# Attention scores of two heads together, with the low key part on 64 rows of the array per head

## The chip, the cores and the metric

The program runs on one core of one Trainium2 chip. The metric is the device time of one execution in microseconds (us), as the median of several runs. TensorE (PE) multiplies; it loads weights in instructions of its own (PEld in the profile). VectorE (DVE), ScalarE (ACT) and GpSimd (POOL) work beside it, and SyncE (SP) issues most of the DMAs.

## What is computed

A network of two transformer blocks and a third mixer, on 1024 tokens of width 1024. The first block has a windowed attention (layer A below: 16 query heads on 4 key heads, a band of 128 keys to each side, and a sink), the second a dilated attention (layer B: three groups of 8 query heads on 2 key heads, dilations 1, 4 and 16). Each is followed by a gated feed-forward net, and then comes a mixer of a state-space model and a short convolution. What matters here is the scores in the attentions, cut from the reference:

```python
def banded_attention(q, k, v, half_window, slopes, dist_scale, sink=None):
    ...
    s = jnp.einsum('nbqhgd,nbkhd->nbhgqk', qb, kw,
                   preferred_element_type=jnp.float32) * (dh ** -0.5) + bias
    s = jnp.where(mask[None, :, None, None], s, NEG)
    m = s.max(axis=-1)
    ...
    p = jnp.exp(s - m[..., None])
    l = p.sum(axis=-1)
    ...
    o = jnp.einsum('nbhgqk,nbkhd->nbqhgd', p, vw.astype(jnp.float32))
```

A head has 64 channels (`dh`), so a score is a sum over 64 products.

## The kernel before

**Two parts for each number.** All large products are made in fp32r, with each operand cut into a high part and the rest, the low part. Projections take three products (`mm3`, L571 to L578: high by high, high by low, low by high).

**Scores.** As a head has 64 channels and the array 128 rows, both parts of a query stand in one tile: `Q[i]` has the high part on rows 0 to 63 and the low part on rows 64 to 127 (written in `q_proj`, L682 and L686). `K1` has the high part of the keys on both halves of the rows, `K2` the low part on both. So two matmuls into one PSUM bank make a head's scores (`Block.score`, L113 and L114): `Q` by `K1` gives high by high plus low by high, and `Q` by `K2` gives high by low plus low by low. The query tile of 128 by 128 is the weight; 192, 256 or 384 columns of keys stream past it. All 128 rows are used in both matmuls.

**Blocks.** A `Block` is 128 queries of four heads that share their keys. Layer A has 32 blocks (4 key heads by 8), with 384 keys, and 256 in the first and last block of a key head. Layer B has 48 (6 units by 8), with 256 keys, and 192 in the first and last block of a unit of dilation 1. So there are 80 blocks, 320 heads, and 640 score matmuls. After its scores, a head goes through DVE (L117: PSUM plus bias into SBUF, with the maximum), ACT (L126: exponential, with the sum), in layer A POOL (L136: division by the sum), PE again (L756: transposes into PSUM), ACT and DVE (L759, L760: the two parts of the weights `pt`) and PE (L770: product with the values `V`). The scores' PSUM banks have the tag `sc`, of which there are two.

**Order.** `attend` (L709) issues the scores of heads 0 and 1, then some matmuls of a projection that has nothing to do with the block (`fill`; lines L590 to L592 and, in the end of layer A, L821 to L823), the scores of heads 2 and 3, the transposes of the block before, and so on. A scheduler then sets the final order of each engine's instructions from priorities and its own estimates, and can put a matmul of another chain between two score matmuls. In the last blocks of layer B there is hardly anything to fill with.

**Matmuls on 64 rows** are already there in small number. The transposes of the values (L658) read rows 64 to 127, and in the first and last block of a unit of dilation 1 the product with the 64 outer values (`vx`, in L770) uses rows 0 to 63. In the order of the kernel before there are 20 stretches of matmuls on fewer than 128 rows.

Of the kernel before, what the change touches and what calls it, by code (L numbers as in the profile page):

```python
# [28 lines left out]
def fl(t):  # L29
    return t.bitcast(F32)  # L30
# [65 lines left out]
class Block:  # L96
# [10 lines left out]

    def score(self, i):

        nc, w, s = self.net.nc, self.w, self.ss[i]  # L110
        ps = self.net.bank("sc")
        keys = slice(self.k0, self.k0 + self.n)
        nc.tensor.matmul(ps[:, 0:self.n], self.Q[i], self.K1[:, keys], start=True, stop=False)  # L113
        nc.tensor.matmul(ps[:, 0:self.n], self.Q[i], self.K2[:, keys], start=False, stop=True)  # L114
        if self.e:
            nc.gpsimd.tensor_copy(s[:, w:w + 1], self.sink[:, i:i + 1])
        nc.vector.tensor_tensor_reduce(s[:, 0:w], ps[:, self.m0:self.m0 + w], self.bias[i], 1.0,  # L117
                                       self.sink[:, i:i + 1] if self.e else -3.0e38, op0=ALU.add, op1=ALU.max,
                                       accum_out=self.mx[:, i:i + 1])
        if i == 3:  # L120
            self.nm = self.net.small([P, 4], "nm", 3)
            nc.vector.tensor_scalar_mul(self.nm, self.mx, -0.125)  # L122
# [26 lines left out]
class Net:  # L149
# [520 lines left out]
    def q_proj(self, Ws, h, perm, Q, halves_first=False, soon=None):  # L670

        nc = self.nc
        for t, hf in [(t, hf) for hf in range(2) for t in range(2)] if halves_first else [(0, 0), (0, 1), (1, 0), (1, 1)]:
            ps = self.bank("g")
            for _ in self.col_gemm_steps(ps, Ws[t](), h, hf):
                yield
                if soon:
                    soon()
                    soon = None
            src = [perm(ps[64 * i:64 * i + 64], None) for i in range(2)]  # L680
            for i in range(2):
                nc.scalar.copy(perm(Q[2 * t + i][0:64], hf), src[i])  # L682
            yield
            for i in range(2):
                q = Q[2 * t + i]
                nc.vector.tensor_sub(perm(q[64:128], hf), src[i], perm(fl(q[0:64]), hf))  # L686

    def project(self, W, h, perm, res, wide, v_tiles, halves_first=False):

# [19 lines left out]
    def attend(self, blocks, fill):  # L709


        last = None
        for n, block in enumerate(blocks + [None]):
            b = block and block()
            if b:
                b.score(0)
                b.score(1)
            fill(n, 0)
            if b:
                b.score(2)  # L720
                b.score(3)
            if last:
                last.turn()
                last.turn()
            if b:
                b.soft(0)
                b.soft(1)
            fill(n, 1)
            if last:
                last.turn()  # L730
            if b:
                b.soft(2)
                b.soft(3)
            fill(n, 2)
            if b and b.e:
                b.weigh()
            if last:
                last.apply()
            last = b
# [1334 lines left out]
```

## Time and profile before

| | |
|---|---|
| Median of 3 runs | 2753.62 us (2752.54 to 2756.7) |
| The profiled execution | 2757.76 us, with a span of 2756.0 us |
| PE busy over the span | 2593.1 us (94%) |
| Granted TensorE clock, mean | 0.980 |
| Layer A attention, 85 to 390 us | 305 us, PE busy in 290.77 |
| Layer B attention, 1185 to 1535 us | 350 us, PE busy in 316.41 |

The other stages (feed-forward nets, the third mixer) run no score matmul. Matmuls are pipelined: a matmul's time in the profile reaches to the end of its last result, while the next has long begun. What a matmul costs in a full stream is the time from its start to the start of the next one, which is why the rows below are read by their starts.

### The profile page before, as it was taken

The numbers are of one execution on the slowest core, as the hardware profiler recorded it, in microseconds if no ns is written. First come the engines' busy times: TensorE is split into PE (matmuls) and PEld (weight loads), VectorE is DVE, ScalarE is ACT, GpSimd is POOL, SyncE is SP. The second block draws the span as 40 slices with busy tenths as digits, with TensorE's granted clock in tenths as the row PEclk, the third lists the DMA queues.
The fourth block names the chain that finished last, engine by engine and source line by source line (L and its number), as shares of the span: only waits on it lengthen the run. The fifth ranks groups of instructions, "written<-read, shape, count | busy, mean of one in ns | idle before, by whom it ended". The sixth has DMA issues, their size and how long they took to land. (4 is left out here: it accounts for less than half of the span.)

```text
span 2756.0 us, 33954 instructions
## 1 busy us (share of the span) xinstructions
PE 2593.1 (94%) x11966; PEld 2115.1 (77%) x11966; DVE 1899.1 (69%) x3559; ACT 1286.1 (47%) x2416; POOL 376.4 (14%) x506
## 2 busy tenths in 40 slices
PE   4999998999999999988899889999999899999998
PEld 4777676888888788776787668888887777988877
DVE  7788777977775976755667798666656978165355
ACT  4577743433333345568888443333333445123131
POOL 2255521000000000023343200000000102020000
PEclk8999999999999999999999999999999999999999
DMA  7333341544444666311122414222274565161141
GB/s 276 99 93 96 119 123 69 156 142 146 138 138 139 232 200 194 107 39 40 39 55 78 145 59 146 82 86 83 85 244 150 176 199 175 54 180 52 46 144 63
DMA packets 283403, 336.74 MB, mean 122 GB/s; under 512 B 59384, under 2 KB 212704, under 8 KB 282592
## 3 DMA queue, kind: packets, MB, share of 16 engines
q1 hardware_dynamic: 277520, 315.59, 36.4%
q0 software_dynamic: 5312, 18.88, 2.1%
q8 instruction: 94, 1.54, 0.2%
q14 instruction: 77, 0.63, 0.1%
q10 hardware_dynamic: 400, 0.09, 0.0%
HBM read 265.14 MB, written 67.27 MB: 121 GB/s over the span
## 5 line engine op out<-in xcount | busy, mean ns | idle before, releaser
L1188 PE MATMUL psg<-H,wpart 128*128 128x512 f32 x2112 | 504.6, 393 | 14.3 <-ACT H L432 10.0
L1188 PEld LDWEIGHTS psg<-H,wpart 128*128 128x128 f32 x2112 | 397.8, 189 | 103.6 <-ACT H L432 12.8
L1175 ACT CAST wpart<-wraw 128x512 fp32r<-128x512 f32 x264 | 163.3, 622 | 248.3 <-PE pstp L1188 76.4
L1188 PE MATMUL pssc<-H,wpart 128*128 128x512 f32 x1056 | 255.0, 390 | 0.5 <-DVE ev L1208 0.5
L1188 PEld LDWEIGHTS pssc<-H,wpart 128*128 128x128 f32 x1056 | 198.1, 188 | 42.1 <-DVE ev L1208 0.9
L1176 DVE TENSOR_TENSOR wpart<-wraw,wpart 128x512 fp32r<-128x512 f32 x264 | 180.9, 686 | 68.5 <-ACT wpart L1175 66.7
L1325 PE MATMUL psg<-part,wpart 128*128 128x512 f32 x792 | 206.8, 394 | 8.0 <-DVE wpart L1291 3.1
L1325 PE MATMUL pssc<-part,wpart 128*128 128x512 f32 x792 | 207.4, 394 | 5.2 <-DVE ev L1212 3.6
L590 PE MATMUL psg<-hh,wh 128*128 128x512 f32 x480 | 198.5, 414 | 2.2 <-ACT hh L527 1.7
L1290 ACT CAST wpart<-wraw 128x640 fp32r<-128x640 f32 (+1 forms) x132 | 101.0, 765 | 210.7 <-PE psg L1325 101.8
L591 PE MATMUL psg<-hl,wh 128*128 128x512 f32 x480 | 192.6, 401 | 2.0 <-DVE hl L530 1.9
L592 PE MATMUL psg<-hh,wl 128*128 128x512 f32 x480 | 191.8, 400 | 0.0
L1325 PEld LDWEIGHTS psg<-part,wpart 128*128 128x128 f32 x792 | 148.4, 189 | 42.7 <-DVE part L1297 5.5
L126 ACT ACTIVATE s<-s,nm 128x256 f32<-128x256 f32 (+4 forms) x320 | 162.4, 511 | 39.6 <-DVE nm L122 33.1
L1325 PEld LDWEIGHTS pssc<-part,wpart 128*128 128x128 f32 x792 | 148.3, 189 | 39.4 <-DVE ev L1212 4.3
L1291 DVE TENSOR_TENSOR wpart<-wraw,wpart 128x640 fp32r<-128x640 f32 (+1 forms) x132 | 117.7, 892 | 83.4 <-ACT wpart L1290 75.8
L1203 ACT COPY ev<-psg 128x512 f32<-128x512 f32 x132 | 77.4, 588 | 205.1 <-PE psg L1188 141.0
L780 POOL TENSOR_TENSOR o<-o,ob 64x512 f32<-64x512 f32 x80 | 117.3, 1467 | 231.8 <-ACT o L779 221.6
L403 POOL TENSOR_TENSOR nacc<-nacc,nsq 128x512 f32<-128x512 f32 x30 | 40.5, 1350 | 761.8 <-ACT nsq L401 761.5
L1325 PE MATMUL pstp<-part,wpart 128*128 128x512 f32 x528 | 137.9, 393 | 0.0
L1296 ACT CAST part<-a 128x512 fp32r<-128x512 f32 x176 | 108.5, 618 | 58.0 <-PE pssc L1325 17.7
L1297 DVE TENSOR_TENSOR part<-a,part 128x512 fp32r<-128x512 f32 x176 | 119.6, 691 | 19.0 <-ACT part L1296 17.8
(454 smaller groups left out, 5488.8 us busy)
## 6 DMA issues: line engine op xcount, KB each, us to landing
adaw<-in_ada_w_dram SPq DMA_DIRECT2D x96, 512.0 KB, 4.2
wraw<-in_ffn_w_in_dram SPq DMA_DIRECT2D x88, 512.0 KB, 3.9
a<-acts SPq DMA_DIRECT2D x132, 256.0 KB, 4.0
acts<-ev SPq DMA_DIRECT2D x44, 512.0 KB, 2.7
wraw<-in_ffn_w_out_dram SPq DMA_DIRECT2D x44, 384.0 KB, 3.5
xs<-x SPq DMA_DIRECT2D x32, 512.0 KB, 3.5
x<-xs SPq DMA_DIRECT2D x32, 512.0 KB, 5.1
wraw<-in_ffn_w_out_dram SPq DMA_DIRECT2D x44, 320.0 KB, 3.3
```

Source lines behind the costliest of these rows:

```text
L126: self.net.nc.scalar.activation(s[:, 0:w], s[:, 0:w], AF.Exp, bias=self.nm[:, i:i + 1], scale=0.125, accum_out=self.l[:, i:i + 1])
L590: nc.tensor.matmul(ps, hi[:, k, :], xhi, start=(k == 0), stop=False)
L591: nc.tensor.matmul(ps, hi[:, k, :], xlo, start=False, stop=False)
L592: nc.tensor.matmul(ps, lo[:, k, :], xhi, start=False, stop=(k == KT - 1))
L780: nc.gpsimd.tensor_add(oap, oap, b)
L1175: nc.scalar.copy(t[:, lo_half], src)
L1176: nc.vector.tensor_sub(t[:, hi_half], src, fl(t[:, lo_half]))
L1188: nc.tensor.matmul(bank[q, key], a[:, ks], b, start=first and k == m == 0, stop=k == 3 and m == 2, skip_group_check=not first)
L1291: nc.vector.tensor_sub(lo, t[:, 0:n], fl(hi))
L1296: nc.scalar.copy(o[:, lo_half], a)
L1297: nc.vector.tensor_sub(o[:, hi_half], a, fl(o[:, lo_half]))
L1325: nc.tensor.matmul(banks[m], a[:, ms], b, start=k == n == 0, stop=k == NK - 1 and n == 2)
```

## The change

For two heads at a time, the two products with `K1` come first, into two banks, and then the two products with `K2`. The latter use only the high part of the query: 64 rows of the weight and 64 rows of the keys. So that the two heads use different halves of the array, the tile of the first head keeps its high part on rows 0 to 63, and that of the second now has it on rows 64 to 127, with the low part on the other half. (`K1` has the same on both halves, so the first product doesn't change.) The product of the low part of the query with the low part of the keys is left out. The number of instructions is the same: 640 score matmuls, of which 320 are now on 64 rows. `score` is called once for two heads, and what followed the matmuls stands in `keep`.

```diff
     def score(self, i):
+        nc, w = self.net.nc, self.w
+        keys = slice(self.k0, self.k0 + self.n)
+        ps = [self.net.bank("sc") for _ in range(2)]
+        for j in range(2):
+            nc.tensor.matmul(ps[j][:, 0:self.n], self.Q[i + j], self.K1[:, keys], start=True, stop=False)
+        for j in range(2):
+            r = slice(64 * j, 64 * j + 64)
+            nc.tensor.matmul(ps[j][:, 0:self.n], self.Q[i + j][r], self.K2[r, keys], start=False, stop=True)
+        for j in range(2):
+            self.keep(i + j, ps[j])
+
+    def keep(self, i, ps):
         nc, w, s = self.net.nc, self.w, self.ss[i]
-        ps = self.net.bank("sc")
-        keys = slice(self.k0, self.k0 + self.n)
-        nc.tensor.matmul(ps[:, 0:self.n], self.Q[i], self.K1[:, keys], start=True, stop=False)
-        nc.tensor.matmul(ps[:, 0:self.n], self.Q[i], self.K2[:, keys], start=False, stop=True)
...
-                nc.scalar.copy(perm(Q[2 * t + i][0:64], hf), src[i])
+                nc.scalar.copy(perm(Q[2 * t + i][64 * i:64 * i + 64], hf), src[i])
...
-                nc.vector.tensor_sub(perm(q[64:128], hf), src[i], perm(fl(q[0:64]), hf))
+                nc.vector.tensor_sub(perm(q[64 - 64 * i:128 - 64 * i], hf), src[i], perm(fl(q[64 * i:64 * i + 64]), hf))
...
                 b.score(0)
-                b.score(1)
             fill(n, 0)
             if b:
                 b.score(2)
-                b.score(3)
```

In the changed kernel the two score matmuls are L116 (with `K1`, 128 rows) and L119 (with `K2`, 64 rows), and the lines behind them are 8 to 10 later: L590 to L592 become L600 to L602, L756 becomes L764, L770 becomes L778.

On PE, at the first two heads of a block of layer A, the order before is this. `K_120` is `K1` and `K_121` is `K2` of the key head, `Q_472` and `Q_473` are the tiles of two heads, and each `pssc` is a bank.

```order
L770 MATMUL pso_1137<-pt_1120,V_575 128x512 x2
L113 MATMUL pssc_1152<-K_120_476,Q_472 128x384
L114 MATMUL pssc_1152<-K_121_477,Q_472 128x384
L113 MATMUL pssc_1157<-K_120_476,Q_473 128x384
L114 MATMUL pssc_1157<-K_121_477,Q_473 128x384
L590 MATMUL psg_1066<-hh_442,wh_815 128x512
```

The order after, on PE at the same place:

```order
L778 MATMUL pso_1137<-pt_1120,V_575 128x512 x2
L116 MATMUL pssc_1152<-K_120_476,Q_472 128x384
L116 MATMUL pssc_1153<-K_120_476,Q_473 128x384
L119 MATMUL pssc_1152<-K_121_477,Q_472 128x384
L119 MATMUL pssc_1153<-K_121_477,Q_473 128x384
L600 MATMUL psg_1066<-hh_442,wh_815 128x512
```

The four matmuls still stand together; the two on 64 rows (L119) have come side by side, between matmuls on 128 rows.

On PE two blocks later, at heads 2 and 3 of a block with 256 keys, the order before:

```order
L113 MATMUL pssc_1372<-K_120_476,Q_474 128x256
L114 MATMUL pssc_1372<-K_121_477,Q_474 128x256
L756 MATMUL pstp_1384<-ident,s_1251 128x128
L113 MATMUL pssc_1377<-K_120_476,Q_475 128x256
L114 MATMUL pssc_1377<-K_121_477,Q_475 128x256
```

And after:

```order
L116 MATMUL pssc_1372<-K_120_476,Q_474 128x256
L119 MATMUL pssc_1372<-K_121_477,Q_474 128x256
L764 MATMUL pstp_1384<-ident,s_1251 128x128
L764 MATMUL pstp_1392<-ident,s_1251 128x128
L116 MATMUL pssc_1373<-K_120_476,Q_475 128x256
L119 MATMUL pssc_1373<-K_121_477,Q_475 128x256
```

Here the scheduler has pulled the two heads apart again: each matmul on 64 rows stands alone between matmuls on 128 rows. Counted through the whole order after, the 320 matmuls L119 stand in 184 stretches on 64 rows (75 in layer A, 109 in layer B): 136 hold both heads of a pair (41 with 384 columns, 90 with 256 and 5 with 192), and 48 hold one head. With the stretches that were there before, some of which have merged with these, there are 196 where there were 20.

## Rows read from the trace of the kernel before

**Rows 1.** Busy time by stretch. The columns are the stretch, its length, then the busy time of PE, PEld, DVE, ACT and POOL with their instructions, the granted share of the TensorE clock, the DMA engines' share and GB/s. The first is the attention of layer A, the third that of layer B.

```profile
85.00:390.00 305.00, 290.77 (x1471) 232.57 (x1470) 243.59 (x532) 204.28 (x479) 148.76 (x288) 0.99 0.36 105
390.00:1185.00 795.00, 770.16 (x3394) 628.06 (x3393) 598.16 (x1080) 327.68 (x528) 35.18 (x30) 0.99 0.47 150
1185.00:1535.00 350.00, 316.41 (x1648) 254.21 (x1646) 222.59 (x602) 284.25 (x659) 115.69 (x86) 0.98 0.20 47
```

**Rows 2.** Who PE waited for, in layer A's stretch and, behind the dots, the longest four of layer B's: in total, times, longest, in us.

```profile
PE pstp L756 <- POOL s L136: 9.6, 23, 1.8
...
PE pso L770 <- DVE pt L760: 9.1, 12, 1.7
PE pssc L113 <- DVE st L117: 9.1, 10, 2.2
PE pso L770 <- ACT pt L759: 5.2, 9, 1.5
PE pssc L113 <- DVE Q L686: 4.5, 6, 1.5
```

**Rows 3.** The timeline of PE alone in layer A: start, duration, line, out<-in, weight and output shapes.

```profile
252.17 0.39 PE L590 MATMUL psg<-hh,wh 128*128 128x512 f32 x1
252.39 0.39 PE L591 MATMUL psg<-hl,wh 128*128 128x512 f32 x1
252.62 0.40 PE L592 MATMUL psg<-hh,wl 128*128 128x512 f32 x1
252.86 0.33 PE L113 MATMUL pssc<-K,Q 128*128 128x384 f32 x1
253.03 0.34 PE L114 MATMUL pssc<-K,Q 128*128 128x384 f32 x1
253.21 0.33 PE L113 MATMUL pssc<-K,Q 128*128 128x384 f32 x1
253.38 0.33 PE L114 MATMUL pssc<-K,Q 128*128 128x384 f32 x1
253.56 0.39 PE L590 MATMUL psg<-hh,wh 128*128 128x512 f32 x1
```

**Rows 4.** The same view in layer B.

```profile
1325.18 0.28 PE L113 MATMUL pssc<-K,Q 128*128 128x256 f32 x1
1325.30 0.28 PE L114 MATMUL pssc<-K,Q 128*128 128x256 f32 x1
1325.42 0.28 PE L113 MATMUL pssc<-K,Q 128*128 128x256 f32 x1
1325.54 0.29 PE L114 MATMUL pssc<-K,Q 128*128 128x256 f32 x1
1325.66 0.40 PE L590 MATMUL psg<-hh,wh 128*128 128x512 f32 x1
```

**Rows 5.** The timeline of PE at two places where one matmul on 64 rows (`vx`, shape 64*128) stands between matmuls on 128 rows.

```profile
1493.42 0.39 PE L592 MATMUL psg<-hh,wl 128*128 128x512 f32 x1
1493.74 0.49 PE L770 MATMUL pso<-pt,vx 64*128 64x512 f32 x1
1494.16 0.38 PE L113 MATMUL pssc<-K,Q 128*128 128x256 f32 x1
1494.38 0.28 PE L114 MATMUL pssc<-K,Q 128*128 128x256 f32 x1
...
1536.42 0.40 PE L576 MATMUL pstp<-oh,wohi 128*128 128x512 f32 x1
1536.74 0.49 PE L770 MATMUL pso<-pt,vx 64*128 64x512 f32 x1
1537.17 0.50 PE L577 MATMUL pstp<-ol,wohi 128*128 128x512 f32 x1
1537.50 0.39 PE L578 MATMUL pstp<-oh,wolo 128*128 128x512 f32 x1
```

**Rows 6.** The weight loads (PEld) at the first of those places, with the idle time of the loads ahead of one, and what ended it, in brackets.

```profile
1493.18 0.19 PEld L592 LDWEIGHTS psg<-hh,wl 128*128 128x128 f32 x1
1493.73 0.18 PEld L770 LDWEIGHTS pso<-pt,vx 64*128 64x128 f32 x1 [0.36 <-ACT pt L759]
1494.16 0.19 PEld L113 LDWEIGHTS pssc<-K,Q 128*128 128x128 f32 x1 [0.24 <-issue]
```

**Rows 7.** The timeline of PE at a place where two matmuls on the same 64 rows follow each other (x2), then two on 128 rows.

```profile
1444.88 0.40 PE L592 MATMUL psg<-hh,wl 128*128 128x512 f32 x1
1445.20 0.73 PE L770 MATMUL pso<-pt,vx 64*128 64x512 f32 x2
1445.86 0.73 PE L770 MATMUL pso<-pt,V 128*128 128x512 f32 x2
1446.43 0.28 PE L113 MATMUL pssc<-K,Q 128*128 128x256 f32 x1
```

**Rows 8.** The timeline of PE at scores with 192 columns in layer B.

```profile
1479.27 0.25 PE L113 MATMUL pssc<-K,Q 128*128 128x192 f32 x1
1479.35 0.28 PE L114 MATMUL pssc<-K,Q 128*128 128x192 f32 x1
1479.47 0.28 PE L113 MATMUL pssc<-K,Q 128*128 128x192 f32 x1
1479.58 0.28 PE L114 MATMUL pssc<-K,Q 128*128 128x192 f32 x1
```

## The prediction, made before the changed kernel ran

> **What bounds the kernel now.** I began with the busy time by stretch, since the change touches the two attentions alone [rows 1]. The reader is to see two things there. In both stretches PE is the fullest engine: 290.77 of 305 us in layer A, with DVE next at 243.59, and 316.41 of 350 us in layer B, with ACT next at 284.25. And PE's idle time is small: 305 - 290.8 = 14.2 us in A and 350 - 316.4 = 33.6 us in B, 47.8 us together. The view of waits says who ends that idle time: POOL's division ahead of the transposes in A, and in B the two parts of `pt` ahead of the product with the values, and DVE's emptying of a score bank ahead of the next score [rows 2]. So work that is added to PE's stream or taken from it counts nearly in full, apart from what falls into those 47.8 us.
>
> Then I took the timelines of PE, to price a matmul by the distance between starts. With 512 columns that is 0.23 us (252.17 to 252.86 for three), with 384 columns (253.56 - 252.86) / 4 = 0.175 us [rows 3], with 256 columns (1325.66 - 1325.18) / 4 = 0.12 us [rows 4], and with 192 columns (1479.58 - 1479.27) / 3 = 0.10 us [rows 8].
>
> **What a stretch on 64 rows costs.** The kernel before already has a few matmuls on 64 rows, and this is the view that decides. Between L592 and L114 stand one such matmul and one score matmul: 1494.38 - 1493.42 = 0.96 us, where a plain stream would take 0.23 + 0.23 + 0.12 = 0.58 us. That is 0.38 us too much. At the second place it is 1537.50 - 1536.42 = 1.08 us for three matmuls of 0.23 us, 0.39 us too much [rows 5]. Where two matmuls on the same 64 rows follow each other, it is 1446.43 - 1444.88 = 1.55 us for five of 0.23 us, 0.40 us too much [rows 7]. So the price hangs on the stretch, not on how many matmuls it holds: about 0.39 us.
>
> The weight loads show how it comes about [rows 6]. In a plain stream the load for the next matmul begins with the present one. The load for the 64-row matmul begins 1493.73 - 1493.42 = 0.31 us after the start of L592, that is 0.08 us after the next start would have been due; nothing of it lies under L592, and the matmul is recorded with 0.49 instead of 0.39 us, so 0.10 us of load stand ahead of its columns. The same on the way back: the load of L113 begins 0.42 us after L770's record, with 0.24 us of idle time that the profile puts to "issue", so to no awaited data. About half the price is paid on entering, half on leaving.
>
> **The change, part by part.**
>
> *Stretches.* The order after has 196 stretches on fewer than 128 rows, 20 before: 176 more. At 0.39 us that is 176 x 0.39 = 68.6 us on PE. All stand in the score matmuls, in the two stretches where PE is the bound.
>
> *Columns saved.* No matmul goes away and none gets fewer columns; 320 use half the rows. Alone such a matmul gains nothing: on 64 rows with 512 columns it is recorded at 0.49 us, 0.10 of it the load, like one on 128 rows [rows 5]. A gain can come only from the 136 stretches that hold both heads, if the second matmul, on the other half of the rows, runs beside the first. No row of before shows two matmuls on different halves. The bounds: nothing, if they run one after the other; and one whole distance for each pair if they run fully together, 41 x 0.175 + 90 x 0.12 + 5 x 0.10 = 18.5 us. Between the two I take the row of 192 columns: those start every 0.10 us, no quicker than the 0.10 us which a load takes where it stands alone [rows 8, 5]. If the second matmul's load comes behind the first's, it starts 0.10 us after it, and a pair saves 0.175 - 0.10 = 0.075 us at 384 columns, 0.02 at 256 and nothing at 192: 41 x 0.075 + 90 x 0.02 = 4.9 us. I take 4.9, for it is the rate that loads show here. A matmul on 64 rows with 256 columns lasts hardly longer than its load.
>
> *Waits for banks.* The `K1` matmul of the second head now stands ahead of the `K2` matmul of the first. If its bank isn't yet emptied by DVE, PE's queue waits one matmul earlier than before, with the first head's `K2` product behind it. Ten waits for that release are seen in B, 9.1 us [rows 2]. Each can get longer by the 0.12 us matmul that stood ahead: 10 x 0.12 = 1.2 us. DVE gets the first head's scores later, but there the second head's follow at once; DVE isn't the bound.
>
> *Query tiles.* ACT and DVE write the same elements to other rows, in the same number of instructions: nothing.
>
> *PE's stream:* 68.6 - 4.9 + 1.2 = 65 us more, with bounds of 51 (18.5 saved) and 70 (nothing saved).
>
> *What the idle time takes.* Some of this falls where PE would have waited anyhow. The division by POOL and the `pt` of a block are waited for after the scores of the next block have gone through PE, so a stretch there runs while the awaited chain runs; but a stretch in the block's own scores makes that same chain start later, and so does every later one on it. Of the 47.8 us I take a third, 16 us; the bounds are nothing and two thirds, 32 us.
>
> *Sum:* 65 - 16 = 49 us. The profiled execution of 2757.8 us would become 2807. It lies 4.1 us above the median of 2753.6, which gives 2803 us. This is the forecast: slower by 1.8%. A difference of 0.2% (5.5 us) is about what a measurement of this kernel can tell from none.
>
> **The rivals.**
>
> *Pairs run fully together.* Then 18.5 us are saved: 68.6 - 18.5 + 1.2 - 16 = 35 us, or 2789 us. Against it speaks the distance of 0.10 us at 192 columns [rows 8]; for it, that this row shows loads into the same rows of the array, not into two halves. The Trainium skill says so (TensorE: Matmul & The Clock Gate, "The mechanism" in Part 3): matmuls on different row groups start some 4 ns apart, with the loads overlapping. By that rule the time would be this rival's. No run here shows it yet.
>
> *Nothing falls into idle time.* If every stretch delays the chain that PE later waits for, the full 65 us remain: 2819 us. For it speaks layer B, where PE waits for results of its own earlier matmuls; against it, that every block has other chains to give way.
>
> *The two halves drain between themselves.* If going from rows 0 to 63 to rows 64 to 127 costs as much as half a stretch, 0.19 us, 136 pairs pay another 26 us: 2829 us. The row of two matmuls in one stretch has the same rows twice and can't tell [rows 7]. The Trainium skill (TensorEngine Tiling (Array Packing), "Key Properties") speaks against it: a change of the tiling mode drains TensorE, a change of the tile alone does not.
>
> *Faster: the 0.39 us is the price of awaited data, not of the rows.* The entering load is put down to ACT [rows 6], and if the new matmuls, whose operands lie ready, pay nothing, the full overlap leaves 18.5 us, or 2735 us. It decides from a price below 18.5 / 176 = 0.105 us for a stretch. Against it: three places of different surroundings show 0.38 to 0.40 us, and the way out, which waits for no data, pays half. That the change doesn't do what it says, with pairs that pay nothing and save only the 4.9 us, gives no change, 2749 us.
>
> **How the numbers follow.** Forecast 0.52; fully together 0.20; nothing into idle time 0.13; drain between halves 0.07; faster 0.05; no change 0.03. The range goes from 51 - 32 = 19 us more (2773) to 70 us more (2824), 2774 to 2824; it leaves out the last three, 0.15. Faster 0.05, same 0.03, slower 0.92.
>
> **What would show it.** Right: in the timeline, the first L119's load begins some 0.3 us after the start of the last L116, a load on 128 rows follows the last L119 with idle time put to "issue", and a pair with both halves, from the first L116 to the matmul behind it, takes about 0.39 us more than four distances, less 0.02 to 0.075. PE's idle time in the two stretches falls from 47.8 to about 32 us while the stretches grow by some 20 us in A and 30 us in B; the rest stays as it is. Wrong: L119's loads lying under the matmul ahead (the faster rival); a second L119 that starts together with the first (fully together); or 0.19 us between the two beyond the load (drain between halves).

## The result, and the profile after

The changed kernel takes 2781.67 us (median of 4 runs, 2778.91 to 2788.02) where the kernel before took 2755.16 us in the same series: a ratio of 1.0101, 95% interval 1.0082 to 1.0120. It is slower by 1.0%, 26.5 us. The forecast was 2803 us (49 us slower), with a range of 2774 to 2824. The way and the price of a stretch were right; two other terms were mis-sized, and the forecast loss is nearly twice the measured one.

The busy time by stretch, of the kernel after. The stretches run to the same places of the program as [rows 1]: the last score of layer A starts 5.2 us later than before, the first of layer B 2.3 us, and the last of layer B 23.2 us.

```profile
85.00:395.20 310.20, 302.50 (x1470) 225.14 (x1469) 238.82 (x531) 204.32 (x479) 146.07 (x287) 0.99 0.35 103
395.20:1187.30 792.10, 768.03 (x3397) 625.45 (x3396) 598.09 (x1080) 328.61 (x529) 35.48 (x31) 0.99 0.48 150
1187.30:1558.20 370.90, 345.18 (x1647) 257.64 (x1645) 219.17 (x601) 286.02 (x660) 115.91 (x87) 0.96 0.19 44
```

Layer A went from 305 to 310.2 us, the part between from 795 to 792.1, layer B from 350 to 370.9; the forecast was some 20 us more in A and 30 in B. So four fifths of what the two attentions lose is in layer B, though 75 of the 184 stretches stand in layer A. Not all of that is the change: the granted clock of layer B's stretch is 0.96 here and 0.98 in [rows 1]. From the first score to the last, the missing share of the clock times the length is 12.0 us here and 6.8 us before, so up to some 5 us of the 20.9 can be the clock (an estimate). It doesn't come with the stretches, for the traces of two kernels below with as many or more of them show 5.1 us (both heads on the same half) and 1.7 us (each head a stretch of its own). PE's idle time fell in A from 14.2 to 310.2 - 302.5 = 7.7 us and in B from 33.6 to 25.7.

The waits of PE in the same two stretches answer to [rows 2]; behind the dots is layer B:

```profile
PE pstp L764 <- POOL s L146: 6.0, 11, 1.7
...
PE pso L778 <- DVE pt L768: 6.5, 9, 1.7
PE pssc L116 <- DVE st L127: 6.2, 8, 2.0
PE pssc L116 <- DVE Q L696: 3.0, 3, 1.2
...
PE pso L778 <- ACT pt L767: 2.5, 3, 1.4
```

Each of the five has become shorter: 9.6 to 6.0 us for POOL, 9.1 to 6.5 for DVE's `pt`, 9.1 to 6.2 for the bank, 4.5 to 3.0 for `Q` and 5.2 to 2.5 for ACT's `pt`.

The timeline of PE at a pair of heads in layer A, which answers to [rows 3] (equal instructions are merged, x2):

```profile
253.25 0.39 PE L602 MATMUL psg<-hh,wl 128*128 128x512 f32 x1
253.48 0.51 PE L116 MATMUL pssc<-K,Q 128*128 128x384 f32 x2
253.92 0.45 PE L119 MATMUL pssc<-K,Q 64*128 64x384 f32 x2
254.29 0.50 PE L600 MATMUL psg<-hh,wh 128*128 128x512 f32 x1
254.63 0.39 PE L601 MATMUL psg<-hl,wh 128*128 128x512 f32 x1
```

And the weight loads there, which answer to [rows 6]:

```profile
253.26 0.41 PEld L116 LDWEIGHTS pssc<-K,Q 128*128 128x128 f32 x2
253.92 0.18 PEld L119 LDWEIGHTS pssc<-K,Q 64*128 64x128 f32 x2 [0.25 <-issue]
254.29 0.19 PEld L600 LDWEIGHTS psg<-hh,wh 128*128 128x128 f32 x1 [0.19 <-issue]
254.40 0.19 PEld L601 LDWEIGHTS psg<-hl,wh 128*128 128x128 f32 x1
```

The reader is to see three things. The loads of L119 and of L600 both wait with 0.25 and 0.19 us of idle time put to "issue": the way in and the way out. From the first L116 to L601 are 1.15 us; four distances of 0.175 and one of 0.23 would be 0.93, so the pair pays 0.22 us net: the stretch's 0.39 less one whole distance of 0.175. And two L119 together last 0.45 us, where one alone takes 0.43 (the rows of "Each head a stretch of its own" below): they run beside each other, their loads too (0.18 us for both). In the trace the second L119 starts 0.003 to 0.004 us behind the first in all 123 pairs that stand directly behind their two L116 (87 with 256 columns, 32 with 384, 4 with 192). Where two products of 512 columns follow such a pair without a wait, the net price read in this way has a median of 0.22 us at 384 columns (16 places) and 0.26 us at 256 (43 places): 0.39 less the whole distance of 0.175 or 0.12.

### The profile page after: what moved, and what is told of

Its sections match the earlier page's. It is cut to its first block, busy times and chain, and to the rows that moved or that the text cites. A ratio compares the mean times of both kernels' runs of the same rounds, so it can differ in the third digit from the quotient of the medians.

```text
span 2779.8 us, 33949 instructions
## 1 busy us (share of the span) xinstructions
PE 2633.2 (95%) x11966; PEld 2109.7 (76%) x11966; DVE 1891.1 (68%) x3559; ACT 1289.5 (46%) x2416; POOL 373.6 (13%) x506
## 5 line engine op out<-in xcount | busy, mean ns | idle before, releaser
L600 PE MATMUL psg<-hh,wh 128*128 128x512 f32 x480 | 207.0, 432 | 2.2 <-ACT hh L537 1.7
L601 PE MATMUL psg<-hl,wh 128*128 128x512 f32 x480 | 193.0, 402 | 1.8 <-DVE hl L540 1.8
L602 PE MATMUL psg<-hh,wl 128*128 128x512 f32 x480 | 192.6, 401 | 0.0
L767 ACT CAST pt<-pstp 128x512 fp32r<-128x512 f32 x168 | 93.2, 588 | 88.9 <-PE pstp L764 87.9
```

Source lines behind the costliest of these rows:

```text
L600: nc.tensor.matmul(ps, hi[:, k, :], xhi, start=(k == 0), stop=False)
L601: nc.tensor.matmul(ps, hi[:, k, :], xlo, start=False, stop=False)
L602: nc.tensor.matmul(ps, lo[:, k, :], xhi, start=False, stop=(k == KT - 1))
```

## The experiments

The sum of the prediction had three terms that could be tested apart: the price of stretches, what a pair saves, and what PE's waits take up. For each kernel, PE's stream is worked out as in the prediction, by its own order: 0.39 us for each stretch more than 20, less a whole distance for each pair that stands together.

### The new order with all rows

```diff
         for j in range(2):
-            r = slice(64 * j, 64 * j + 64)
-            nc.tensor.matmul(ps[j][:, 0:self.n], self.Q[i + j][r], self.K2[r, keys], start=False, stop=True)
+            nc.tensor.matmul(ps[j][:, 0:self.n], self.Q[i + j], self.K2[:, keys], start=False, stop=True)
```

> The new order (both K1 products first, then both K2 products, two banks taken together) and the new query tiles, but the K2 products on all 128 rows: no stretch on 64 rows is added (20 as in the kernel before). Theory: the loss is the price of the stretches, so this is as the kernel before, 2755 us, within 5 us. Rival: the loss comes from the order and from PE's queue waiting for the second bank; then this stays at 2770 us or more.

Measured: 1.0014 of the kernel before (1.0003 to 1.0024), 2759.8 us. The order, the two banks taken together and the new tiles cost some 4 us, by the interval 1 to 7, and a part of it may be the clock (0.9774 on the mean of these runs, 0.9786 in those of the kernel before). By the traces PE's instructions stand here in exactly the order of the changed kernel, so the 22 us between the two come with the rows alone. The timeline of PE (L118 is the product with `K2` here):

```profile
251.28 0.51 PE L116 MATMUL pssc<-K,Q 128*128 128x384 f32 x2
251.63 0.52 PE L118 MATMUL pssc<-K,Q 128*128 128x384 f32 x2
251.99 0.40 PE L599 MATMUL psg<-hh,wh 128*128 128x512 f32 x1
```

Four matmuls in 0.71 us. In the changed kernel it is 253.48 to 254.29, and 0.10 us of load before L600's columns begin: 0.91 us.

### Both heads on the same half

```diff
-            r = slice(64 * j, 64 * j + 64)
+            r = slice(0, 64)
...
-                nc.scalar.copy(perm(Q[2 * t + i][64 * i:64 * i + 64], hf), src[i])
+                nc.scalar.copy(perm(Q[2 * t + i][0:64], hf), src[i])
...
-                nc.vector.tensor_sub(perm(q[64 - 64 * i:128 - 64 * i], hf), src[i], perm(fl(q[64 * i:64 * i + 64]), hf))
+                nc.vector.tensor_sub(perm(q[64:128], hf), src[i], perm(fl(q[0:64]), hf))
```

> As the changed kernel, but both heads keep their high query part on rows 0 to 63, so the two K2 products of a pair use the same rows and can't run side by side. 184 stretches as before, 197 in all. Theory: a pair on two halves runs fully together, so this loses up to one distance for each of 136 pairs, 18.5 us of PE's stream, of which some falls into waits: 2790 to 2800 us, and the second L119 starts 0.12 (256 columns) or 0.175 us (384) after the first instead of 0.003. Rival, as I had predicted: a pair saves only 4.9 us; then at most 2787 us.

Measured: 1.0131 (1.0111 to 1.0151), 2788.3 us, 6.6 us above the changed kernel. The time alone lies between the two expectations (2787 and 2790 us), and the trace decides. The timeline of PE, then that of the loads:

```profile
255.46 0.51 PE L116 MATMUL pssc<-K,Q 128*128 128x384 f32 x2
255.90 0.61 PE L119 MATMUL pssc<-K,Q 64*128 64x384 f32 x2
256.44 0.73 PE L778 MATMUL pso<-pt,V 128*128 128x512 f32 x2
```

```profile
255.90 0.29 PEld L119 LDWEIGHTS pssc<-K,Q 64*128 64x128 f32 x2 [0.25 <-issue]
256.44 0.30 PEld L778 LDWEIGHTS pso<-pt,V 128*128 128x128 f32 x2 [0.25 <-issue]
```

Here the second load runs behind the first (0.29 us for both in place of 0.18), and the load on the way out begins 0.54 us after the first L119, in the changed kernel 0.37 us: the two halves do save a whole distance of 0.17 us for a pair. The second L119 starts 0.22 us (256 columns) or 0.28 us (384) after the first, 0.10 us more than I expected, since the first one's record begins with 0.10 us of load. So the two halves save 18.5 us of PE's stream, of which 6.6 us (by the ratios 8 us) show in the time; the intervals of the two ratios allow 1 to 16 us.

### Each head a stretch of its own

```diff
-        nc.tensor.matmul(ps[:, 0:self.n], self.Q[i], self.K2[:, keys], start=False, stop=True)
+        nc.tensor.matmul(ps[:, 0:self.n], self.Q[i][0:64], self.K2[0:64, keys], start=False, stop=True)
```

> The order of the kernel before, head by head, with each K2 product on rows 0 to 63 as a stretch of its own: 332 stretches, 312 more than before, and no pair. PE's stream gets 312 x 0.39 = 122 us longer. Theory: PE's waits take up some 25 to 35 us and no more, the rest counts in full: 2840 to 2850 us. Rival: the waits always take about half, as in the changed kernel (50 us of stream, 26 us of time): 2815 us.

Measured: 1.0224 (1.0202 to 1.0245), 2815.2 us. My expectation was wrong and the rival's right: 61 us of time for 122 us of stream. That it fits to the microsecond is luck, as the interval is 56 to 67 us. PE's order is that of the kernel before, instruction for instruction. The timeline of PE in layer A:

```profile
259.54 0.33 PE L113 MATMUL pssc<-K,Q 128*128 128x384 f32 x1
259.80 0.43 PE L114 MATMUL pssc<-K,Q 64*128 64x384 f32 x1
260.16 0.44 PE L113 MATMUL pssc<-K,Q 128*128 128x384 f32 x1
260.54 0.43 PE L114 MATMUL pssc<-K,Q 64*128 64x384 f32 x1
260.90 1.09 PE L756 MATMUL pstp<-ident,s 128*128 128x128 f32 x8
```

From the first L113 to the columns of L756 (0.05 us after the record's start at 260.90, its load: the eight last 1.09 us here and 1.04 us in a plain stream of the kernel before, at 1327.51) are 1.41 us, four distances are 0.70: two stretches cost 0.71 us, 0.36 each, a little under 0.39; why is not shown. At the 16 places of this trace where a stretch of 256 or 384 columns is followed, with no wait in view, by two matmuls on all rows of which the first is no transpose, the price is 0.38 to 0.40 us. So the price holds, and it is the waits that take more than I had allowed.

### Pairs held together

```diff
+        mm = []
         for j in range(2):
-            nc.tensor.matmul(ps[j][:, 0:self.n], self.Q[i + j], self.K1[:, keys], start=True, stop=False)
+            mm.append(nc.tensor.matmul(ps[j][:, 0:self.n], self.Q[i + j], self.K1[:, keys], start=True, stop=False))
         for j in range(2):
             r = slice(64 * j, 64 * j + 64)
-            nc.tensor.matmul(ps[j][:, 0:self.n], self.Q[i + j][r], self.K2[r, keys], start=False, stop=True)
+            mm.append(nc.tensor.matmul(ps[j][:, 0:self.n], self.Q[i + j][r], self.K2[r, keys], start=False, stop=True))
+            self.net.pin(mm[-1])
```

> The changed kernel with the K2 products tied to their program order behind both K1 products, so that the scheduler pulls fewer pairs apart: 165 stretches with K2 products in place of 184, 155 of them with both heads (136), 178 stretches in all. PE's stream is 158 x 0.39 - 21 = 41 us longer than before, in place of 50. Theory: 2773 to 2778 us. Rival: the scheduler pulled pairs apart where PE waited for a bank anyhow, and holding them together costs as much in waits: 2782 us or more.

Measured: 1.0072 (1.0057 to 1.0086), 2775.0 us, as the theory had it. Fewer stretches and more pairs help, but even with nearly all pairs together the change loses 0.7%.

### The change in one layer alone

```diff
+            if not (self.e):
+                nc.tensor.matmul(ps[j][:, 0:self.n], self.Q[i + j], self.K2[:, keys], start=False, stop=True)
         for j in range(2):
             r = slice(64 * j, 64 * j + 64)
-            nc.tensor.matmul(ps[j][:, 0:self.n], self.Q[i + j][r], self.K2[r, keys], start=False, stop=True)
+            if self.e:
+                nc.tensor.matmul(ps[j][:, 0:self.n], self.Q[i + j][r], self.K2[r, keys], start=False, stop=True)
```

`self.e` is 1 in layer A alone. For layer B the two conditions are exchanged. In the layer without the change, each head's two products are issued one after the other, as in the kernel before.

> The change in layer A alone (layer B with the K2 products on all 128 rows): 94 stretches, 74 more than before. PE's stream is 74 x 0.39 - 41 x 0.175 - 12 x 0.12 = 20 us longer. Theory: PE's waits ahead of the transposes take most of it in A, so 2757 to 2763 us. Rival: added work on PE counts in full, 2775 us.

> The change in layer B alone: 123 stretches, 103 more than before. PE's stream is 103 x 0.39 - 78 x 0.12 - 5 x 0.10 = 30 us longer. Theory: two thirds of it stay, since in B PE waits for results of its own chain: 2772 to 2779 us. Rival: the waits take half as everywhere, 2768 us or less. With the change in layer A alone, the two sums should make the whole change's 26 us within 5 us.

Measured: layer A alone 1.0023 (1.0012 to 1.0034), 6 us for 20 us of stream; layer B alone 1.0069 (1.0049 to 1.0088), 19 us for 30. Together 25 us, the whole change's 26.5 within the intervals. By these middle values a third of the stream's cost shows in A and two thirds in B. The intervals, 3 to 9 us of 20 and 13 to 24 us of 30, just touch as shares, and the runs of layer B alone had a lower granted clock (0.977 on the mean, 0.9785 in those of the kernel before), so the times alone don't prove the difference between the layers.

### Layer A without the division

The first kernel is the kernel before without these lines of `attend`, the second the change in layer A alone without them:

```diff
-            if b and b.e:
-                b.weigh()
```

> The kernel before without the division by the sums in layer A (POOL's tensor_scalar and DVE's reciprocal left out; the output of layer A is then not normalised). PE's waits for POOL ahead of the transposes go away. Theory: layer A gets shorter by a good part of what PE loses ahead of the transposes, 2730 to 2748 us. Rival: something else is late there at once, and the time stays at 2750 us or more. It is the base for the next kernel.

> The change in layer A alone, also without the division (left out as in the kernel ahead): 92 stretches, 20 us more of PE's stream than in the kernel ahead. Theory: it was the waits for POOL that hid the change in layer A; with them gone the 20 us count nearly in full, 14 to 22 us over the kernel ahead. Rival: PE's waits take the same share whatever they are for, 8 us or less over the kernel ahead.

Measured: 0.9918 (0.9903 to 0.9933) without the division, and 0.9973 (0.9962 to 0.9984) with the change on top, so 1.0055 between the two, 12 us by the medians and 15 by the ratios, in place of 6. By the medians the time stands between my numbers, nearer to the theory's; by the ratios it is the theory's (10 to 20 us by their intervals, against 3 to 9 with the division). The waits of PE in layer A, of the change in layer A alone:

```profile
PE pstp L767 <- POOL s L149: 6.2, 11, 1.6
```

and of the kernel before without the division, then with the change on top:

```profile
PE pstp L754 <- DVE pt L758: 3.7, 7, 0.9
...
PE pstp L765 <- DVE pt L769: 1.9, 5, 0.7
```

With POOL's division there are waits ahead of the transposes that added work can use up (9.6 us in [rows 2], 6.2 with the change); without it, there is less to use (3.7 and 1.9). From the first to the last score of layer A the change adds 280.6 - 268.9 = 11.7 us without the division, and 295.9 - 288.3 = 7.6 us with it.

### The K2 products left out

```diff
-        nc.tensor.matmul(ps[:, 0:self.n], self.Q[i], self.K1[:, keys], start=True, stop=False)
-        nc.tensor.matmul(ps[:, 0:self.n], self.Q[i], self.K2[:, keys], start=False, stop=True)
+        nc.tensor.matmul(ps[:, 0:self.n], self.Q[i], self.K1[:, keys], start=True, stop=True)
```

> The kernel before with the 320 K2 products left out altogether (the low part of the keys is not multiplied at all, so the scores are less exact). No stretch on 64 rows is added. PE's stream is 96 x 0.175 + 208 x 0.12 + 16 x 0.10 = 43 us shorter: all that any saving on the low part could bring. Theory: as with added work, about half of it shows, because PE then waits longer for the same chains: 2728 to 2738 us. Rival: it shows in full, 2712 us.

Measured: 0.9913 (0.9899 to 0.9928), 24 us less for 43 us of stream. This is what leaving out the low key part altogether gives in this order, and it too shows by about half.

### The division shared with ACT

Since the waits for POOL turned out to cost time, two kernels give a part of the division to ACT, without the change (`n` is 3 for one head on ACT, 2 for two):

```diff
-            nc.gpsimd.tensor_scalar(self.ss[i][:, 0:w], self.ss[i][:, 0:w], rl[:, i:i + 1], 1.0, op0=ALU.mult, op1=ALU.mult)
+            if i < n:
+                nc.gpsimd.tensor_scalar(self.ss[i][:, 0:w], self.ss[i][:, 0:w], rl[:, i:i + 1], 1.0, op0=ALU.mult, op1=ALU.mult)
+            else:
+                nc.scalar.activation(self.ss[i][:, 0:w], self.ss[i][:, 0:w], AF.Copy, scale=rl[:, i:i + 1])
```

> The kernel before, with the division by the sums for one head of four in layer A on ACT instead of POOL (the same computation). POOL's chain ahead of the transposes gets a quarter shorter. Theory: of the 26 us that PE loses ahead of the transposes in layer A, some 5 to 10 us go: 2743 to 2749 us. Rival: ACT's queue is longer by one instruction a block, and what stands behind it (the copies of the transposes) comes later: 2753 us or more.

> The same with two heads of four on ACT. Theory: POOL's chain is half as long, so 2738 to 2747 us, if ACT, with 204 us busy of 305 in layer A, has room for 64 more instructions of some 0.6 us. Rival: ACT now holds up the transposes' copies, 2750 us or more.

Measured: 0.9961 (0.9948 to 0.9975) with one head on ACT and 0.9952 (0.9939 to 0.9965) with two, 2744.6 and 2741.8 us. Both beat the kernel before, and so the changed one. The busy time in layer A with two heads on ACT:

```profile
85.00:376.00 291.00, 283.39 (x1469) 231.19 (x1468) 235.62 (x531) 232.94 (x541) 109.03 (x225) 1.00 0.36 110
```

ACT went from 204 to 233 us and POOL from 149 to 109, and the layer from 305 to some 291 us.

## Why the prediction was right in its way and wrong in its size

**What bounds the kernel** held in part. The loss lies in the two attentions, where PE's stream got longer; the part between them differs by 3 us. But that added work "counts nearly in full" did not hold: about half of it shows (below), and in layer A work taken from POOL makes the kernel faster, with nothing taken from PE.

**The price of a stretch** held: 0.39 us, half on entering and half on leaving, in the new stretches as in the old ones. It isn't the price of awaited data, so the rival on the faster side falls: the profile puts the idle time ahead of L119's loads to "issue", and the same order with all rows doesn't pay it.

**What a pair saves** was mis-sized. I took the load as the rate, with the second matmul 0.10 us behind the first, and 4.9 us in all. Measured: 0.003 us between the starts, the loads beside each other as well, and so the whole 18.5 us. The row of 192 columns, on which I rested, shows loads one after the other into the same rows; the experiment with both heads on the same half shows just that again (0.29 us for two loads, 0.18 on two halves). I named this limit of the row and still chose by it. The rival "pairs run fully together" was right in this step. The Trainium skill's sentence (TensorE: Matmul & The Clock Gate, "The mechanism") agrees with the trace: some 4 ns there, 3 to 4 ns here. With 0.003 us between the two halves there is no drain between them, and that rival falls. The Trainium skill says the same of a change of the tile alone (TensorEngine Tiling (Array Packing), "Key Properties"), and the trace agrees.

**The waits for banks** (1.2 us) can't be told from nothing: the visible ones got shorter, and the new order with all rows costs some 4 us, with this term and all else in it.

**What the idle time takes** was mis-sized. I allowed a third of 47.8 us, 16 us. Worked out from the two measured prices, PE's stream is 68.6 - 18.5 = 50 us longer; the time is 26.5 us longer, so 24 us were taken up. Two things were wrong in the step. The idle time of the view fell much as forecast, from 47.8 to 33.4 us (forecast: about 32), but it is not all that PE loses, for a matmul is recorded until its results are out, 0.33 us for 384 columns that start every 0.175 us [rows 3]; a wait of up to 0.16 us is hidden in it. Summed over the starts instead, as distance less the plain distance for the width (0.109 us for the transposes), PE lost 34 us in layer A and 58 us in layer B of the kernel before, 92 us in place of the 46 that show as waits there. (Up to some 10 us of it is time at a granted clock under 1, 0.99 and 0.98 in [rows 1], and not waits.) In A 26 of these stand ahead of the transposes; after the change it is 15, and with each head a stretch of its own 9. And no fixed sum is taken up, as I had it: over all kernels that moved the stream in both layers, the time follows it by about half. By the medians 41 us gave 20 (pairs held), 50 gave 26.5, 69 gave 34 (same half), 122 gave 61, and -43 gave -24. This is shown for these kernels. The first three have the new order too, whose 4 us are in these times.

That the rest falls into waits can be read from the traces by itself. Leave out the distances up to a matmul on 64 rows, and take the price of the way out off the two distances behind one: then PE loses 32 us in layer A and 52 in layer B of the kernel before, and 17 and 39 after the change. That is 28 us less, near the 24 which the sum leaves over. With each head a stretch of its own it is 10 and 16, so 57 us less, where 61 of 122 don't show in the time. The same estimate gives 13 of 20 us taken up with the change in layer A alone, 10 of 30 with it in layer B alone, and without the division, where there were only 12.5 us to use in layer A, 6.5 of 20. So waits which the added work fills are shown as the cause for layer A, by the two kernels without the division; for layer B they are read from the traces, and no run takes its waits away. Why the sum comes out so near to one half is open.

**The sum:** 49 us predicted, less 13.6 (pairs) and some 8 (waits), and 1.2 for the banks: 26. The 8 us are what the measured time leaves for the waits, so it is no check that this sum closes; the check is the 28 us from the traces.

## What to carry to other kernels

Matmuls on the two halves of the rows ran two at a time here, in full, but each excursion to them among matmuls on all rows had a price that did not depend on how many it held. It was 0.39 us, against 0.12 to 0.175 us saved per pair: by these numbers (an estimate, no run here has such an order) one excursion has to hold more than three pairs of 256 columns before it pays, and a scheduler that pulls pairs apart makes it worse. Before taking waits as small because the busiest engine shows little idle time, sum up the distances of its starts: the records of matmuls that overlap hide waits, and these waits shrink both the cost of added work and the gain of removed work.

## What the runs showed of the hardware

Two weight loads into the two halves of the rows start 0.003 us apart and take 0.18 us together, while two into the same half take 0.29 us. I had expected that loads always follow each other. And the price of a stretch hardly depends on what is in it: 0.38 to 0.40 us with one matmul [rows 5], with two on the same rows [rows 7] or with two on different halves; the lowest that the rows shown here give is 0.36 us, on the mean of two stretches with one matmul between them and transposes behind.
